# A conditioned two-layer decoder step: x loaded ahead of the first modulation weights, softmax's masked copy scaled by -1/8 with a minimum that starts at the negated sink, and another block order

## The chip, the cores and the metric

One Trainium2 chip, one of its cores. The metric is the device time of one execution in microseconds. A core has TensorE (PE, the matrix products; "PEld" is its weight load), VectorE (DVE), ScalarE (ACT), GpSimd (POOL), a queue engine SyncE (SP) that here only starts transfers, and 16 DMA engines that carry the transfers between HBM and the on-chip memory SBUF. Products land in PSUM, eight banks of 2 KB per partition.

## The reference, cut to what matters

512 prompt tokens and 8 x 8 sample tokens go through two layers of width 1024, in float32.

```python
for l in range(DEPTH):                       # DEPTH = 2
    sh1, sc1, g1, sh2, sc2, g2 = split(silu(c) @ ada_w[l] + ada_b[l], 6)
    h = rms_norm(x, norm_g[l, 0]) * (1 + sc1) + sh1
    out = recurrent_block(h, ...) if l < 1 else attention(h @ attn_w_q, k, v) @ attn_w_o
    x = x + g1 * out
    h = rms_norm(x, norm_g[l, 1]) * (1 + sc2) + sh2
    x = x + g2 * swiglu(h, ffn_w_in[l], ffn_w_out[l])
    if l == 0: k, v = shared keys and values from the modulated norm of x
y = rms_norm(x, final_g)
```

Recurrent block: `xr, yg = split(h @ w_in)`, a causal convolution of width 4 on `xr`, two sigmoid gates from 8 blocks of 128 x 256, a linear recurrence with `a = exp(8 r log_sigmoid(lambda))`, times `gelu(yg)`, `@ w_out`. Attention: 16 heads of 64 over 4 key heads, a window of 128, and a learned sink in the softmax:

```python
s = where(mask, q @ k.T / 8, -1e30)
m = maximum(max(s), sink)
p = exp(s - m) / (sum(exp(s - m)) + exp(sink - m))
```

## The kernel before

**Tiling.** The 576 tokens are two halves of 288 (256 prompt and 32 sample tokens), A (h = 0) and B (h = 1), with features on the partitions, eight columns c of 128 features. Each float32 operand is split into a rounded high part and the low rest, so a block of 128 x 128 weights times a half is three products of 128 x 288 (high-high, high-low, low-high). Weights come as units of 512 KB into `raw` buffers; ScalarE copies the high part, VectorE subtracts for the low part (buffers `wh`). `x0` to `x7` are the units of `rnn_w_in`'s first half, `y0` to `y7` of the second, `g0` to `g7` the gates of block c.

**Order.** The program is recorded first: each engine call is an entry with a cost from a table (`Engine.record`), and `Recorder.schedule` puts the entries in an order per engine by those costs. All entries are issued from one line, L447, so every row of the profile has that line. The strings `RNN` and `ATT` give the order in which the blocks of the recurrent layer and of attention are recorded (q: query columns, a: attention of a chunk of prompt heads, s: one sample's attention, f: its end, o: output columns; A and B are the halves). `early(n)` moves an entry n places up in priority.

**Front.** SP's queue loads c, x (tile 4 is the samples, tiles 0 to 3 the prompt), vectors and weights in the recorded order. `x_half` squares and sums x for the norm and turns its tiles by transposes on TensorE. `ada_first(c)` computes shift and scale (SH1, SC1) of the first layer for two columns: 32 matmuls of 128 columns into an `ada` bank, from 2 MB of `ada_w` that `ada_first_load` brings, a copy, a transpose, `ada_end` for bias and gain (`mods`). Then `modulated` makes `x * rstd` (VectorE and GpSimd), scales and shifts it (ScalarE, into `tb`), and splits it into `h`. Four such stages of two columns follow each other; tiles 2 and 3 of x are loaded behind the first stage's weights. The other modulations are computed later, spread among the products, in 512-wide matmuls from `reg` buffers. `decay_rates` computes log_sigmoid of lambda on VectorE by powers of two and series.

**Softmax.** `attn_chunk(c)` takes two heads (j) and two token blocks (b) of a half. Scores are masked and their maximum found by one reduction on VectorE; then follow the scaled minimum with the negated sink (`nm`), the sink's exponent argument, Exp on ScalarE with its sum, and the division. `attn_sample` does it for one sample with the sink as an extra column.

Of the kernel before, what the change touches and what calls it, by code (L numbers as in the profile page):

```python
# [12 lines left out]
F32 = mybir.dt.float32  # L13
# [26 lines left out]
ST = (1, 1, 1)  # L40
EW = EP = EA = EK = E1 = ER = 0
# [11 lines left out]
ATT = ("q0A a0A q1A q2A q0B a1A q1B a0B a2A q3A q2B a1B a3A q3B q4A q4B a2B q5A a4A a3B q6A a5A q5B a4B "  # L53
       "q7A a6A q6B a5B s0A s1A a7A s2A s3A q7B s0B a6B fA a7B o0A s1B s2B o1A s3B o2A fB")
# [324 lines left out]
class Engine:  # L379
# [8 lines left out]
    def record(self, name, args, kw):  # L388
# [18 lines left out]
        if name == "matmul":  # L407
# [9 lines left out]
            if first.ap[0][1] == 32 and args[1].ap[0][1] == P and n >= P:  # L417
                cost = n / 2.4 + 30 if dt == F32 else n / 9.6 + 15
                mode = 3
        elif name == "transpose":  # L420
            cost = 107.0
        elif name == "dma_start":
            src = args[1]
            n = max(_free(first) * first.ap[0][1], _free(src) * src.ap[0][1])
            cost, lat = (460.0 if eng == "SP" else 1020.0), n * 4 / 335.0 + 5
# [21 lines left out]
        self.rec.add(eng, lambda: getattr(obj, name)(*map(real, args), **{k: real(v) for k, v in kw.items()}), cost, outs, ins, func, lat, port, mode)  # L447

# [25 lines left out]
def trunk_kernel(ctx, tc, a):  # L474
# [123 lines left out]
    for t in (4, 0, 1):  # L598
        x_load(t)
# [44 lines left out]
    def decay_rates():  # L644
        tw = sl()
        z, neg, msk, scl, p_, w_, w2, s_ = [tw.f[:, 8 * i : 8 * i + 8] for i in range(8)]
        V.tensor_scalar(hgb[:], vecT[:, 80:96], 0.5, None, ALU.mult)
        V.tensor_scalar(neg, lamT, -1.0, None, ALU.mult)
        V.tensor_tensor(z, lamT, neg, ALU.max)
        V.tensor_scalar(z, z, 87.0, None, ALU.min)  # L650
        V.memset(scl, 1.0)
        for kk in (64, 32, 16, 8, 4, 2, 1):
            V.tensor_scalar(msk, z, kk * math.log(2.0), None, ALU.is_ge)
            V.scalar_tensor_tensor(z, msk, -kk * math.log(2.0), z, ALU.mult, ALU.add)
            V.tensor_scalar(w_, msk, -1.0, 1.0, ALU.mult, ALU.add)
            V.scalar_tensor_tensor(w_, msk, 2.0 ** -kk, w_, ALU.mult, ALU.add)
            V.tensor_tensor(scl, scl, w_, ALU.mult)
        V.memset(p_, 1.0)
        for n in range(11, 0, -1):
            V.scalar_tensor_tensor(p_, p_, -1.0 / n, z, ALU.mult, ALU.mult)  # L660
            V.tensor_scalar(p_, p_, 1.0, None, ALU.add)
        V.tensor_tensor(p_, p_, scl, ALU.mult)
# [4 lines left out]
        V.memset(s_, 1.0 / 17)  # L667
        for n in range(15, 0, -2):
            V.tensor_tensor(s_, s_, w2, ALU.mult)
            V.tensor_scalar(s_, s_, 1.0 / n, None, ALU.add)  # L670
        V.scalar_tensor_tensor(s_, s_, 2.0, w_, ALU.mult, ALU.mult)
        V.scalar_tensor_tensor(s_, neg, 0.0, s_, ALU.max, ALU.add)
# [20 lines left out]
    def ada_turn(o, n):  # L693

        t = aux()
# [20 lines left out]
    def ada_first_load(c, kind):  # L716

        first_w[c] = []
        for q in range(4):
            b = kind(F32) if kind is whs else kind()  # L720
            first_w[c].append(b)
            for g in (SH1, SC1):
                w, o = ada_w(g)
                src = w[q * 2 * P : (q + 1) * 2 * P, o + c * P : o + (c + 2) * P].rearrange("(k p) n -> p k n", p=P)
                Q.dma_start(b.f[:, 512 * g : 512 * g + 512].rearrange("p (k n) -> p k n", k=2), src)

    def ada_first(c):
        o = ps(pada, "ada")
        for q, b in enumerate(first_w[c]):
            for k in range(2):  # L730
                ada_mm(o, 2 * q + k, [b.f[:, n : n + P] for n in (256 * k, 256 * k + P, 512 + 256 * k, 512 + 256 * k + P)], q + k == 0, q + k == 4)
            b.done()
        t = ada_turn(o, 1)[:, 0:P].rearrange("p (g c b) -> p g c b", g=2, c=2)
        for g in (SH1, SC1):
            ada_end(g, slice(c, c + 2), t[:, g, :, 0:9])
# [1266 lines left out]
```

## Time and profile before

| | |
|---|---|
| median of 3 runs | 1262.42 us (1261.84 to 1265.04) |
| the profiled execution's own time | 1263.01 us |
| its span | 1261.2 us |
| TensorE busy | 1237.8 us |
| VectorE, ScalarE, GpSimd busy | 920.3, 663.1, 252.7 us |
| moved by DMA | 165.38 MB, mean 131 GB/s |

A row of the timeline has start, duration, engine, line, operation, output <- inputs by the program's names, shape, count, and in brackets the idle time ahead of it with what ended it. A window's row has the stretch, then for PE, PEld, DVE, ACT and POOL the busy time and number of instructions, then the granted TensorE clock, the DMA engines' busy share and GB/s. A row of groups has the count, busy time, mean ns of one, and idle time before. A row of waits has the total, the number and the longest. Matmuls are pipelined and their ends are modelled, so times of single ones overlap; the starts are measured.

### The profile page before, as it was taken

The page shows a single profiled execution, that of the slowest core. Times are in us where ns is not written, and L with a number is a line of the kernel's source. Part 1 is how long each engine was busy: PE and PEld are TensorE (multiplying, and loading weights), DVE is VectorE, ACT ScalarE, POOL GpSimd, SP SyncE. Part 2 cuts the span into 40 slices and gives each one's busy share as a digit, 9 for nine tenths or more (in the row PEclk, how much of TensorE's full clock was granted, in tenths as well). Part 3 has the DMA queues.
Part 4 walks back from the last instruction along what each step waited for, and adds up shares of the span by engine and source line. Part 5 has one row for each costly group of instructions (what it writes and reads, how often), then busy time and mean ns, then how long its engine had stood idle before and what let it go on. Part 6 is the DMA issues. An engine that isn't in the chain of part 4 may idle for free.

```text
span 1261.2 us, 25276 instructions
## 1 busy us (share of the span) xinstructions
PE 1237.8 (98%) x9532; PEld 1166.9 (93%) x9532; DVE 920.3 (73%) x2283; ACT 663.1 (53%) x1498; POOL 252.7 (20%) x542
## 2 busy tenths in 40 slices
PE   7999999999999999999999999999999999999997
PEld 5798999899899899989998997999999999999997
DVE  6998784795577468656778887558957865875776
ACT  4788973764255335514567678538523542552442
POOL 3456351101100010011024335100011011001011
PEclk8999999999999999999999999999999999999999
DMA  9955554535456655464513220332342232332322
GB/s 306 318 179 188 188 177 151 170 86 171 140 152 191 185 167 184 156 194 137 167 33 75 68 60 27 111 97 97 85 133 68 84 110 76 90 100 80 100 69 76
DMA packets 219755, 165.38 MB, mean 131 GB/s; under 512 B 23629, under 2 KB 204841, under 8 KB 219602
## 3 DMA queue, kind: packets, MB, share of 16 engines
q1 hardware_dynamic: 219186, 163.45, 43.0%
q8 instruction: 75, 1.23, 0.4%
q0 software_dynamic: 448, 0.32, 0.1%
q14 instruction: 46, 0.38, 0.1%
HBM read 160.85 MB, written 4.87 MB: 131 GB/s over the span
## 4 chain that ended last, share of the span: by engine, by line
PE 86%; DVE 6%; ACT 4%; DMA 2%; POOL 1%; issue 1%; SPq 0%; ACTq 0%; DVEq 0%
PE mm L447 82%; PE ada L447 4%; DVE wh L447 1%; DVE ta L447 1%; ACT tb L447 1%; DVE sl L447 1%; ACT ta L447 1%; DVE tb L447 1%; ACT h L447 1%; DMA raw<-in_rnn_w_in_dram 1%; ACT wh L447 1%; POOL h L447 1%; DMA reg<-in_ada_w_dram 1%; ACT sl L447 1%; DMA reg<-in_x_prompt_dram 1%
## 5 line engine op out<-in xcount | busy, mean ns | idle before, releaser
L447 PE MATMUL mm<-h,wh 128*128 128x288 f32 x4128 | 596.2, 298 | 3.8 <-ACT h L447 1.8
L447 PEld LDWEIGHTS mm<-h,wh 128*128 128x128 f32 x4128 | 560.5, 188 | 23.2 <-issue 11.3
L447 PE MATMUL mm<-sl,wh 128*128 128x288 f32 x3218 | 460.6, 296 | 0.4 <-ACT sl L447 0.3
L447 ACT CAST wh<-raw 128x512 fp32r<-128x512 f32 (+2 forms) x380 | 269.1, 721 | 345.7 <-PE mm L447 208.9
L447 PEld LDWEIGHTS mm<-sl,wh 128*128 128x128 f32 x3218 | 436.6, 188 | 9.0 <-issue 5.9
L447 DVE TENSOR_TENSOR wh<-raw,wh 128x512 fp32r<-128x512 f32 (+2 forms) x380 | 310.2, 828 | 59.3 <-ACT wh L447 57.0
L447 DVE SCALAR_TENSOR_TENSOR x<-mm,mods,x 128x256 f32<-128x256 f32 x160 | 77.0, 482 | 136.1 <-PE mm L447 136.0
L447 POOL TENSOR_TENSOR td<-td,td 128x288 f32<-128x288 f32 x38 | 35.5, 934 | 475.8 <-ACT td L447 467.7
L447 POOL TENSOR_TENSOR x<-x,ta 128x32 f32<-128x32 f32 x152 | 55.3, 364 | 331.1 <-DVE ta L447 325.9
L447 PE MATMUL mm<-tb,wh 128*128 128x288 f32 (+1 forms) x488 | 88.5, 296 | 0.4 <-ACT td L447 0.4
L447 PEld LDWEIGHTS mm<-tb,wh 128*128 128x128 f32 x488 | 72.4, 188 | 1.9 <-DVE sl L447 0.8
L447 ACT COPY td<-mm 128x288 f32<-128x288 f32 (+2 forms) x140 | 49.0, 364 | 37.7 <-DVE mm L447 18.0
L447 DVE TENSOR_TENSOR raw<-raw,raw 128x512 f32<-128x512 f32 x76 | 61.4, 808 | 0.9
L447 PE MATMUL mm<-ta,wh 128*128 128x288 f32 (+1 forms) x254 | 56.1, 298 | 0.0
L447 ACT ACTIVATE ta<-x 128x288 f32<-128x288 f32 x56 | 24.8, 444 | 55.6 <-POOL x L447 52.4
L447 DVE TENSOR_TENSOR raw<-raw 128x512 f32<-128x512 f32 x76 | 52.2, 688 | 1.1
L447 DVE TENSOR_TENSOR td<-mm,td 128x288 f32<-128x288 f32 x76 | 34.5, 454 | 23.4 <-PE mm L447 23.3
L447 PE MATMUL ada<-reg,cz 128*32 128x512 f32 (+1 forms) x448 | 49.5, 553 | 0.0
L447 PEld LDWEIGHTS mm<-ta,wh 128*128 128x128 f32 x254 | 41.7, 188 | 1.8 <-ACT wh L447 0.8
L447 ACT ACTIVATE ta<-ta,stat 128x128 f32<-128x128 f32 (+2 forms) x72 | 32.3, 471 | 18.5 <-DVE stat L447 17.7
L447 DVE TENSOR_TENSOR acc<-acc,ta 128x288 f32<-128x288 f32 x54 | 25.1, 464 | 12.4 <-ACT ta L447 12.4
L447 ACT CAST sl<-ta 128x288 fp32r<-128x288 f32 x54 | 23.0, 431 | 18.5 <-DVE ta L447 18.5
(202 smaller groups left out, 1197.9 us busy)
## 6 DMA issues: line engine op xcount, KB each, us to landing
raw<-in_ffn_w_in_dram SPq DMA_DIRECT2D x88, 512.0 KB
reg<-in_ada_w_dram SPq DMA_DIRECT2D x80, 512.0 KB
raw<-in_ffn_w_out_dram SPq DMA_DIRECT2D x48, 384.0 KB
raw<-in_rnn_w_in_dram SPq DMA_DIRECT2D x16, 512.0 KB
reg<-in_kv_ada_w_dram SPq DMA_DIRECT2D x16, 512.0 KB
wh<-in_ada_w_dram SPq DMA_DIRECT2D x24, 256.0 KB
raw<-in_rnn_w_out_dram SPq DMA_DIRECT2D x8, 512.0 KB
raw<-in_ffn_w_out_dram SPq DMA_DIRECT2D x8, 512.0 KB
```

The lines of the kernel that those rows point to most:

```text
L447: self.rec.add(eng, lambda: getattr(obj, name)(*map(real, args), **{k: real(v) for k, v in kw.items()}), cost, outs, ins, func, lat, port, ...
```

## The change

1. **x first.** All five tiles of x are loaded and turned ahead of the first modulation weights, and `X0` holds `x * rstd` for all columns before shift and scale are known (`modulated` then runs with `known=True`).
2. **The first modulation in three stages** (`FIRST`): columns 0 to 3 at once from 4 MB in rows of 2 KB, 32 matmuls of 256 columns, then columns 4 and 5, and 6 and 7, as before. The matmuls of a stage stay together by `FQ`. Their transposes go to the `ada` banks.
3. **Units.** x0 to x3 are loaded as pairs of two columns by half the rows (`unit_two`, rows of 1 KB), and the gates as two units of four blocks instead of two units by gate (`ug`). `linear_two` is the product over such a pair.
4. **Decay rates** by ScalarE's Exp and a shorter series.
5. **Softmax.** The reduction adds the mask, scales by -1/8, and takes the minimum from the negated sink on, so it gives `nm` directly; Exp then has scale -1. The sink's argument for both token blocks is one subtraction.
6. **Another order**: `ATT`, the recorder's costs of narrow float32 matmuls and of transfers by row length, and priorities (`E1`).

SP's queue at the start (`wh_` and `reg_` are buffers; the last figures are partitions, blocks and columns), before:

```order
L447 DMA reg_108<-in_x_sample_dram 64x1024
L447 DMA reg_111<-in_x_prompt_dram 128x1024
L447 DMA reg_113<-in_x_prompt_dram 128x1024
L447 DMA sl_116<-in_ada_b_dram 96x128
L447 DMA sl_118<-in_norm_g_dram 32x128
L447 DMA wh_121<-in_ada_w_dram 128x2x256 x2
L447 DMA wh_127<-in_ada_w_dram 128x2x256 x2
L447 DMA wh_137<-in_ada_w_dram 128x2x256 x2
L447 DMA wh_147<-in_ada_w_dram 128x2x256 x2
L447 DMA raw_160<-in_rnn_w_in_dram 128x8x128
L447 DMA reg_166<-in_x_prompt_dram 128x1024
```

and after:

```order
L453 DMA reg_107<-in_x_prompt_dram 128x1024
L453 DMA reg_109<-in_x_prompt_dram 128x1024
L453 DMA reg_112<-in_x_prompt_dram 128x1024
L453 DMA reg_114<-in_x_prompt_dram 128x1024
L453 DMA sl_117<-in_ada_b_dram 96x128
L453 DMA sl_120<-in_norm_g_dram 32x128
L453 DMA raw_124<-in_rnn_w_in_dram 128x4x256
L453 DMA wh_131<-in_ada_w_dram 128x2x512
L453 DMA wh_135<-in_ada_w_dram 128x2x512
L453 DMA wh_140<-in_ada_w_dram 128x2x512
L453 DMA wh_146<-in_ada_w_dram 128x2x512
```

Two tiles of x and the first weight unit moved ahead of the modulation weights; the first stage's eight loads are of 512 KB instead of 256 KB.

TensorE around the first products (`mm_349`, `mm_441` and `mm_444` are their PSUM banks, `h_` the modulated half A; `ada_` rows with `cz` are modulation matmuls, rows with `ident` transposes), before:

```order
L447 MATMUL ada_214<-wh_147,cz 32x128 x6
L447 MATMUL mm_308<-ident,ta_304 128x128
L447 MATMUL mm_285<-ident,sl_163 128x96
L447 MATMUL mm_331<-ident,reg_166 128x128 x4
L447 MATMUL mm_337<-ident,reg_166 128x128 x4
L447 MATMUL mm_349<-h_323,wh_314 128x288
L447 MATMUL mm_354<-ident,reg_173 128x128 x4
L447 MATMUL mm_362<-ident,reg_173 128x128 x4
```

and after:

```order
L453 MATMUL ada_302<-wh_166,cz 32x256 x2
L453 MATMUL ada_302<-wh_173,cz 32x256 x2
L453 MATMUL mm_357<-ident,sl_180 128x64
L453 MATMUL ada_393<-ident,ta_385 128x128 x2
L453 MATMUL ada_415<-reg_183,cz 32x128 x8
L453 MATMUL ada_415<-reg_201,cz 32x128 x8
L453 MATMUL mm_441<-h_432,wh_265 128x288
L453 MATMUL mm_444<-h_432,wh_265 128x288
```

Before, one product stands between the transposes of x's tiles 2 and 3, after two columns are modulated; now four columns are, and half of the next stage's modulation matmuls stand ahead of the first product.

VectorE in the first softmax chunk (`stat` holds `nm`, `snk` the sinks; ISA rows are the reduction and the read of its accumulator), before:

```order
L447 ISA ta_9075,stat_96<-mm_9045,reg_7886 128x256
L447 ISA stat_96 128x1
L447 SCALAR_TENSOR_TENSOR stat_96<-stat_96,snk 128x2
L447 ISA tb_9083,stat_96<-mm_9047,reg_7886 128x256
L447 ISA stat_96 128x1
L447 TENSOR_TENSOR stat_96<-stat_96,snk 128x2
```

and after:

```order
L453 ISA ta_8975,stat_96<-mm_8951,reg_7616,snk 128x256
L453 ISA stat_96 128x1
L453 ISA tb_8980,stat_96<-mm_8953,reg_7616,snk 128x256
L453 ISA stat_96 128x1
L453 ISA ta_8985,stat_95<-mm_8961,reg_7616,snk 128x128
```

The scaled minimum and the addition between the reductions are gone, and the reductions read the negated sink.

The diff, cut:

```diff
-ST = (1, 1, 1)
+ST = (2, 1, 2)
+FQ = ((0, 1), (2,), (3,))
+FIRST = ((0, 4), (4, 2), (6, 2))
+E1 = ((400, 200), (0, 0), (0, 0))
-ATT = ("q0A a0A q1A q2A q0B a1A q1B a0B a2A q3A q2B a1B a3A q3B q4A q4B a2B q5A a4A a3B q6A a5A q5B a4B "
-       "q7A a6A q6B a5B s0A s1A a7A s2A s3A q7B s0B a6B fA a7B o0A s1B s2B o1A s3B o2A fB")
+ATT = ("q0A q1A a0A a1A q2A q0B q1B q2B a0B q3A a2A q4A a3A a1B q3B a2B q5A a4A q4B a3B q6A a5A q5B a4B "
+       "q7A a6A s0A q6B a7A s1A s2A s3A a5B q7B s0B a6B fA o0A s1B a7B s2B s3B o1A fB o2A")
...
-    for t in (4, 0, 1):
+    for t in (4, 0, 1, 2, 3):
         x_load(t)
...
+        V.tensor_tensor(p_, lamT, neg, ALU.min)
+        S.activation(p_, p_, AF.Exp)
...
+    def linear_two(us, col, ops, evac):
+        def run(h):
+            o = ps()
+            product(o[:, 0:HC], us[0], ops(h)[0:4], last=False, col=col)
+            product(o[:, 0:HC], us[1], ops(h)[4:8], first=False, col=col)
...
-                    V.tensor_tensor_reduce(out=y[:, 0:W], in0=sc[j][:, 256 * b : 256 * b + W], in1=masks[:, 256 - W : 256], op0=ALU.add, op1=ALU.max,
-                                           scale=1.0, scalar=-1e30, accum_out=mx[:, 2 * b + j : 2 * b + j + 1])
-                V.scalar_tensor_tensor(nm[:, i], mx[:, i], -0.125, nsink[:, 2 * c : 2 * c + 2], ALU.mult, ALU.min)
-                V.tensor_tensor(mx[:, i], nm[:, i], sinks[:, 2 * c : 2 * c + 2], ALU.add)
+                    V.tensor_tensor_reduce(out=y[:, 0:W], in0=sc[j][:, 256 * b : 256 * b + W], in1=masks[:, 256 - W : 256], op0=ALU.add, op1=ALU.min,
+                                           scale=-0.125, scalar=nsink[:, 2 * c + j : 2 * c + j + 1], accum_out=nm[:, k : k + 1])
...
+        X0[h] = [sl() for _ in range(KC + 1)]
+        V.tensor_tensor(X0[h][KC].f[:, 0 : 32 * KC].rearrange("p (c n) -> p c n", c=KC), x[h][:, :, HP:HC], rstd[h][:, HP:HC].unsqueeze(1).to_broadcast([P, KC, 32]), ALU.mult)
+        for c in range(KC):
+            (V, V, G)[c % 3].tensor_tensor(X0[h][c].f[:, 0:HP], x[h][:, c, 0:HP], rstd[h][:, 0:HP], ALU.mult)
...
     x_half(0)
-    ada_first_load(0, whs)
+    x_half(1)
+    load_more(1)
+    ada_first_load(*FIRST[0], whs)
     vectors()
```

168 lines of the change are left out of this document (89 added, 79 removed).

## The prediction

> **What bounds the kernel now.** I read first the page's busy shares and its chain, then the windows of the first 70 us, then TensorE's own timeline there, because the chain says that TensorE is the path almost everywhere.
>
> ```profile
> PE 1237.8 (98%) x9532; PEld 1166.9 (93%) x9532; DVE 920.3 (73%) x2283; ACT 663.1 (53%) x1498; POOL 252.7 (20%) x542
> ...
> PE 86%; DVE 6%; ACT 4%; DMA 2%; POOL 1%; issue 1%; SPq 0%; ACTq 0%; DVEq 0%
> ...
> 245.61 49.69 PE mm L447 x371
> ```
>
> TensorE is busy for 98% of the span, and in a quiet stretch of the chain 371 products take 49.69 us, 0.134 us each. From about 50 us to the end it is fed without pause, so a change can win only where it is not fed: at the start, at a few stage borders, and in attention. The windows give each engine's busy time in 10 us, the granted clock, the DMA share and GB/s:
>
> ```profile
> 0.00:10.00 10.00, 4.69 (x27) 4.17 (x28) 0.97 (x6) 5.10 (x8) 6.12 (x20) 1.00 0.76 234
> 10.00:20.00 10.00, 6.74 (x84) 4.11 (x83) 8.64 (x39) 3.09 (x7) 2.50 (x6) 1.00 1.11 336
> 20.00:30.00 10.00, 9.91 (x84) 7.08 (x82) 8.90 (x31) 6.37 (x14) 2.09 (x5) 0.66 1.11 346
> 30.00:40.00 10.00, 8.01 (x103) 5.50 (x103) 9.27 (x44) 5.07 (x13) 3.08 (x4) 1.00 1.13 327
> 40.00:50.00 10.00, 10.00 (x105) 7.50 (x106) 9.18 (x55) 6.17 (x15) 1.66 (x2) 1.00 1.10 338
> 50.00:60.00 10.00, 9.79 (x72) 7.73 (x71) 9.50 (x25) 9.20 (x27) 5.13 (x13) 1.00 0.97 287
> ```
>
> The DMA engines are full from 10 to 50 us, VectorE is at nine tenths throughout, and TensorE's clock is low between 20 and 30. TensorE's rows of that stretch (start, duration, what, count):
>
> ```profile
> 16.40 0.63 PE L447 MATMUL ada<-wh,cz 128*32 128x128 f32 x12
> ...
> 20.71 0.61 PE L447 MATMUL mm<-h,wh 128*128 128x288 f32 x1
> ...
> 29.14 0.64 PE L447 MATMUL ada<-wh,cz 128*32 128x128 f32 x16
> ...
> 34.81 0.66 PE L447 MATMUL mm<-h,wh 128*128 128x288 f32 x3 [1.57 <-ACT h L447]
> ...
> 46.98 0.63 PE L447 MATMUL ada<-wh,cz 128*32 128x128 f32 x12
> ...
> 56.87 1.93 PE L447 MATMUL ada<-reg,cz 128*32 128x512 f32 x16
> ...
> 74.54 1.93 PE L447 MATMUL ada<-reg,cz 128*32 128x512 f32 x16
> ```
>
> The first product starts at 20.71 and the last columns of the first modulation at 46.98. The second block of 512-wide modulation starts at 74.54; in both orders exactly 237 products stand before it. It is my finish line for the front. Between 20.71 and 74.54 lie 53.8 us for 31.7 us of products (237 x 0.134): the rest is modulation, x's transposes, waits and slow clock.
>
> **The change, part by part.** First the front's start. Ahead of the first product now stand x (0.26 + 4 x 0.52 MB), one weight unit (0.52) and eight modulation loads of 0.52: 7.1 MB, with some 0.3 of vectors 7.4 (before: 4.3). By the windows 2.34 + 3.36 = 5.70 MB pass in 20 us, and the other 1.7 at 346 GB/s need 4.9: 24.9 us. The same count puts the last byte of before's first unit (4.25 MB) at 15.7, and the chain has it landed at 10.72 + 7.41 = 18.13, 2.4 later:
>
> ```profile
> 10.72 7.41 DMA raw<-in_rnn_w_in_dram
> ...
> 28.00:29.00 1.00, 1.00 (x20) 0.77 (x19) 1.00 (x6) 1.00 (x4) 0.00 (x0) 1.00 1.10 354
> ...
> 31.00:32.00 1.00, 0.83 (x18) 0.63 (x18) 0.93 (x6) 0.12 (x1) 0.42 (x1) 1.00 1.18 305
> ...
> 48.00:49.00 1.00, 1.00 (x10) 1.00 (x9) 0.93 (x9) 0.87 (x1) 0.00 (x0) 1.00 1.01 410
> ```
>
> So the last quarter lands at 27.3 if the rate stays. It need not: by the byte count the 28th us carried rows of 1 KB (354 GB/s), the 31st rows of 512 B (305), the 48th rows of 4 KB (410). The change makes the first modulation's rows 2 KB and those of units x0 to x3 and of the gates 1 KB instead of 512 B. At 380, between the two neighbours, the landing is 25.8. I take 26.5; both ends go into the range. The last quarter's 8 matmuls of 256 columns are half of 8 of 512 (1.93 at 56.87), so 1.0: end 27.5. In before the last modulation ended at 17.03 and the first product came 3.7 later, ScalarE's 1.04 us conversion among it; that conversion is now done in the wait, while two more small VectorE steps are added, so 3.4: first product at 30.9 (29.8 to 32.5), ten later than before. Who was waiting on the moved loads: SP's queue now puts x's last two tiles and the unit ahead of all modulation. The unit's load also waits there for a buffer that ScalarE's square of tile 0 frees, and the modulation behind it; over 2 MB of x are then still in flight, so I price that at nothing; with the queue run dry it would be about 1 us.
>
> Then to the finish line: 237 products 31.7; 64 small modulation matmuls (before: 128), 8 per 0.64 (row 29.14, where the profile has two records for each), 5.1, of which 1.3 stands ahead of the first product: 3.8; the first 512-wide block 1.9; transposes 0.4. Sum 37.8, so 68.7 with no wait. x's last transposes and the normalization of x, which stood between products, are hidden under the wait for 4.2 MB. Waits I add: ScalarE feeds two columns in 1.6 us,
>
> ```profile
> 35.11 1.09 ACT L447 ACTIVATE tb<-ta,mods 128x256 f32<-128x256 f32 x2
> 36.11 0.70 ACT L447 CAST h<-tb 128x256 fp32r<-128x256 f32 x2
> 36.71 1.05 ACT L447 CAST wh<-raw 128x1024 fp32r<-128x1024 f32 x1
> ```
>
> (35.11 to 36.71), and 12 products on them take 1.6: even, so about 0.7 for the sample columns. Ahead of columns 4 and 5, ScalarE then has two conversions of 1.05 (row 36.71) and VectorE their two lo parts; VectorE does the second lo part ahead of the step that columns 4 and 5 wait for. Products of other columns cover all but about 1.2. The evacuations of four units at once cost 0.5, a half clock about 0.4. Together 2.8: finish line at 71.5 against 74.54, **gain 3.0**. Ends: 29.8 + 37.8 + 1 = 68.6 (gain 5.9), and 32.5 + 37.8 + 5.7 = 76.0 (loss 1.5), the 5.7 being the 2.8, 1.3 more of half clock and 1.6, as much as the longest wait on ScalarE above (1.57 at 34.81).
>
> What removes the cover of VectorE's decay chain: 80 tiny instructions in three groups, 13.7 us busy,
>
> ```profile
> L447 DVE TENSOR_SCALAR sl<-sl 128x8 f32<-128x8 f32 x35 | 5.8, 166 | 0.3
> ...
> L447 DVE SCALAR_TENSOR_TENSOR sl<-sl 128x8 f32<-128x8 f32 x27 | 4.9, 183 | 0.5
> ...
> L447 DVE TENSOR_TENSOR sl<-sl 128x8 f32<-128x8 f32 x18 | 3.0, 164 | 0.4
> ```
>
> become about 15 of them, roughly 11 us off an engine that was full; no term of its own, it is why I let VectorE keep pace above. ScalarE takes one Exp and a table load, in the wait. Later the order has three table loads fewer (22 to 19), beside full TensorE: 0; were TensorE not fed there, they would be a gain. The split gate units hold two buffers instead of four: 0 for the same reason. The transposes of the first modulation go from the six product banks to the other two: 0, with the products as cover. POOL's queue issues the same loads in the same place. The units of x0 to x3 come as pairs by rows, so x0 and x1 need a second load for columns 4 to 7; it lands after the first half's 48 products can start, and the wait for it is in the 1.2 above.
>
> Softmax: per pair of blocks two scaled minima and two additions go, one addition comes; 40 + 32 - 16 = 56 small ones by 0.187 take 10.4 us off VectorE.
>
> ```profile
> L447 DVE SCALAR_TENSOR_TENSOR stat<-stat,snk 128x2 f32<-128x2 f32 (+1 forms) x40 | 7.1, 183 | 0.0
> ...
> L447 DVE TENSOR_TENSOR stat<-stat,snk 128x2 f32<-128x2 f32 x32 | 6.0, 191 | 0.4
> ...
> 59.79 0.47 DVE L447 TENSOR_TENSOR tb<-sl,ta 128x300 fp32r<-128x300 f32 x1
> 60.17 0.53 DVE L447 SCALAR_TENSOR_TENSOR sl<-td,vecT,sl 128x300 f32<-128x300 f32 x1
> ```
>
> The 72 reductions now read a per-partition start value. No row shows that; the nearest, an instruction with such an operand against one without, is 0.53 to 0.47, so 0.06 each or 4.3 us back; ends 0 and 0.3 (five times that row). TensorE's waits from 640 to 812 us:
>
> ```profile
> PE mm L447 <- DVE wh L447: 1.0, 1, 1.0
> PE mm L447 <- ACT ta L447: 0.8, 1, 0.8
> ...
> PE ada L447 <- ACT td L447: 0.3, 1, 0.3
> ...
> PE mm L447 <- DVE td L447: 0.5, 2, 0.3
> PE mm L447 <- ACT td L447: 0.4, 2, 0.2
> PE mm L447 <- ACT h L447: 0.2, 1, 0.2
> PE mm L447 <- ACT wh L447: 0.2, 1, 0.2
> ```
>
> These are 3.4 us. The first two stand before softmax and stay. A shorter VectorE chain and the new order (a5B and q7B now after the A samples) can take the rest, and unflagged thin spots around 770 to 792 as much again. I take **1.3**; ends 3 and, since an order can also expose a chain, -1.
>
> Sum 4.3 on the profiled execution's 1263.0: 1258.7. That execution stands 0.6 above the median 1262.42, so 1258.1.
>
> [...] The row first: TensorE's granted clock fell to 0.50 after a sparse stretch and came back in the 28th us.
>
> ```profile
> 18.00:19.00 1.00, 0.00 (x0) 0.00 (x0) 0.90 (x5) 0.84 (x1) 0.63 (x2) 1.00 1.05 357
> ...
> 21.00:22.00 1.00, 1.00 (x6) 1.00 (x6) 1.00 (x4) 1.00 (x3) 0.00 (x0) 0.50 1.12 342
> ...
> 27.00:28.00 1.00, 1.00 (x18) 0.50 (x12) 0.93 (x6) 0.37 (x2) 0.00 (x0) 0.81 1.10 351
> ```
>
> The wait for 4.2 MB is longer and sparser: four bursts of 1 us in 17 to 27 us. [...]
>
> **Rivals.** [...] (b) *All covered*: the landing at 25.8 and waits of 1.0: front 5.5, attention 2.4, time 1254.5. For it: 38 us of work for TensorE lie ready between 31 and 69 us. Against: three engines must keep an even pace for that. (c) *It moves the start and not the end*: VectorE (9.50 of 10 from 50 to 60) sets the finish line through conversions and evacuations: gain 0, time 1262.4. Against: 11 us fewer there. (d) *Slower*: the reductions' start value turns them into a slower form. At 0.3 each VectorE gains 21.6 in the attention stage and loses 10.4; it becomes late for the transposes' copies and TensorE waits for most of the 11: 1262.4 - 3.0 + 10 = 1269.4. It decides from about 0.145 each on (10.4 / 72), and the time passes that of before at about 0.19. Against it: the 0.06.
>
> **How the numbers follow.** 0.3% of 1262.4, what a measurement here can tell from no change, is 3.8: faster means under 1258.6, slower over 1266.2. Forecast 0.50, own range 1255.5 to 1260.5, of which 0.30 lie under 1258.6 and 0.20 above; (b) 0.22; (a) 0.15; (c) 0.06; (d) 0.07. Faster 0.30 + 0.22 = 0.52; same 0.20 + 0.15 + 0.06 = 0.41; slower 0.07. The range goes from (b) less 1.0, for both upper ends at once, to (c) plus 0.6, the spread of one execution: 1253.5 to 1263.0.
>
> **What would show it.** Right: first product at 30 to 32.5, the second 512-wide block at 70 to 73, no wait over 1.5 between; decay instructions a quarter; attention's waits under 3 us; the reduction's mean 0.43 at most for 256 columns by the same row kind. Wrong: a first product after 34, clock 0.50 beyond 33, or a wait on VectorE in the first 70 us above 2.

## The result and the profile after

| | before | after |
|---|---|---|
| median | 1262.13 us (1261.72 to 1265.04, 4 runs) | 1253.72 us (1253.59 to 1254.91, 4 runs) |
| ratio | | 0.9931, 95% interval 0.9913 to 0.9948 |
| profiled execution, span | 1263.01, 1261.2 | 1253.59, 1251.6 |

The change is faster by 8.4 us, which is 0.7% and clear of the noise. The forecast gain was 4.3, about half of it; the time lies at the lower end of the range. First the page of the changed kernel, the busy shares and the chain by engine:

```profile
PE 1229.2 (98%) x9468; PEld 1164.5 (93%) x9468; DVE 907.7 (73%) x2144; ACT 657.4 (53%) x1492; POOL 260.6 (21%) x541
...
PE 93%; DVE 4%; ACT 2%; issue 0%; POOL 0%; DMA 0%; ACTq 0%; SPq 0%
```

TensorE is 93% of the chain instead of 86%. VectorE and ScalarE fell from 10% of it to 6, DMA from 2% to 0. Where that happened is seen in the windows of the first 60 us (PE, PEld, DVE, ACT, POOL, then granted clock, DMA share, GB/s):

```profile
10.00:20.00 10.00, 6.82 (x41) 4.96 (x44) 9.46 (x20) 5.38 (x9) 4.53 (x8) 0.81 1.07 365
20.00:30.00 10.00, 8.33 (x97) 4.13 (x90) 9.18 (x44) 3.16 (x10) 1.03 (x3) 0.85 1.08 361
30.00:40.00 10.00, 10.00 (x120) 8.89 (x120) 6.20 (x16) 8.37 (x22) 2.02 (x5) 1.00 1.10 349
40.00:50.00 10.00, 10.00 (x100) 9.63 (x100) 5.65 (x18) 8.09 (x25) 2.30 (x7) 1.00 1.09 360
50.00:60.00 10.00, 10.00 (x77) 8.30 (x76) 9.96 (x20) 9.57 (x22) 8.73 (x15) 1.00 0.90 287
```

From 30 to 50 us TensorE has no gap, and VectorE is busy for 6.20 and 5.65 of 10 us, where before it was 9.27 and 9.18. ScalarE is busier than before: 8.37 and 8.09 instead of 5.07 and 6.17. TensorE's own rows give the milestones: the last quarter of the first modulation, the first product, and the two 512-wide blocks of which the second is the finish line:

```profile
25.06 1.06 PE L453 MATMUL ada<-wh,cz 128*32 128x256 f32 x12 [0.58 <-DMA wh<-in_ada_w_dram]
...
29.25 1.40 PE L453 MATMUL mm<-h,wh 128*128 128x288 f32 x7 [0.60 <-ACT h L453]
...
51.79 1.92 PE L453 MATMUL ada<-reg,cz 128*32 128x512 f32 x16
...
67.83 1.92 PE L453 MATMUL ada<-reg,cz 128*32 128x512 f32 x16
```

The first product starts 8.5 us later than before, the finish line comes 6.7 us earlier. The later stages can be cut where half A's sums for a norm start (six or four matmuls of one column): behind layer 0, behind attention, and before the end. Before:

```profile
643.11 0.73 PE L447 MATMUL mm<-small,acc 128*128 128x1 f32 x6
...
843.57 0.69 PE L447 MATMUL mm<-small,acc 128*128 128x1 f32 x6
...
1235.48 0.56 PE L447 MATMUL mm<-small,acc 128*128 128x1 f32 x4
```

After, the last two of them (the first is at 635.24):

```profile
834.67 0.69 PE L453 MATMUL mm<-small,acc 128*128 128x1 f32 x6
...
1225.32 0.56 PE L453 MATMUL mm<-small,acc 128*128 128x1 f32 x4
```

So the stages of one traced execution each, in us, for all kernels that were run ("layer 0" is the finish line to 643.11, "attention" is with keys and values):

| kernel | front | layer 0 | attention | last feed-forward | end | median |
|---|---|---|---|---|---|---|
| before | 74.54 | 568.57 | 200.46 | 391.91 | 25.7 | 1262.13 |
| before again (e8) | 73.99 | 568.54 | 201.34 | 391.85 | 25.8 | 1262.63 |
| after | 67.83 | 567.41 | 199.43 | 390.65 | 26.3 | 1253.72 |
| after again (e12) | 70.47 | 567.40 | 199.33 | 390.63 | 26.4 | 1254.01 |
| e1 x late | 72.10 | 569.23 | 199.58 | 390.64 | 25.6 | 1258.83 |
| e2 narrow stages | 71.00 | 567.85 | 199.11 | 391.11 | 25.6 | 1256.48 |
| e3 old decay rates | 72.69 | 568.99 | 198.99 | 391.68 | 25.7 | 1258.86 |
| e4 old softmax | 69.77 | 567.34 | 206.32 | 390.93 | 25.6 | 1261.07 |
| e5 old ATT | 68.03 | 567.40 | 216.92 | 390.58 | 25.6 | 1270.67 |
| e6 old costs | 68.71 | 569.58 | 199.16 | 392.19 | 25.6 | 1257.79 |
| e7 old units | 71.16 | 568.66 | 199.63 | 391.81 | 25.5 | 1258.48 |
| e9 old softmax and ATT | 67.71 | 567.37 | 203.22 | 390.99 | 25.6 | 1254.88 |
| e10 before, new softmax | 75.89 | 569.43 | 213.98 | 392.11 | 25.6 | 1277.75 |
| e11 before, new decay | 73.77 | 571.18 | 200.51 | 391.34 | 25.6 | 1264.18 |
| e13 after, filled | 68.14 | 567.56 | 199.22 | 390.70 | 26.3 | 1254.10 |
| e14 before, filled | 73.07 | 569.00 | 200.40 | 391.54 | 25.8 | 1262.49 |
| e15 after, 1 KB rows | 69.93 | 567.38 | 199.04 | 390.63 | 25.6 | 1254.10 |
| e16 after, VectorE late | 71.22 | 567.37 | 199.14 | 390.62 | 25.6 | 1255.45 |

The 9.6 us between the two spans are 6.7 in the front, 1.2 in layer 0, 1.0 in attention, 1.3 in the last feed-forward, less 0.6 at the end. The second traces of the two kernels (e8 and e12) give 3.5 in the front and the same in layer 0 and the feed-forward. Layer 0 and the feed-forward repeat within 0.1 us when a kernel is run again; the front of the changed kernel does not (67.8 and 70.5, see e12), so single fronts of kernels that differ by under 2.6 us are not told apart, and medians are used there.

### The profile page after: what moved, and what is told of

It reads as the page before. It is cut to its first block, busy times and chain, and to the rows that moved or that the text cites. A ratio compares the mean times of both kernels' runs of the same rounds, so it can differ in the third digit from the quotient of the medians.

```text
span 1251.6 us, 25018 instructions
## 1 busy us (share of the span) xinstructions
PE 1229.2 (98%) x9468; PEld 1164.5 (93%) x9468; DVE 907.7 (73%) x2144; ACT 657.4 (53%) x1492; POOL 260.6 (21%) x541
## 4 chain that ended last, share of the span: by engine, by line
PE 93%; DVE 4%; ACT 2%; issue 0%; POOL 0%; DMA 0%; ACTq 0%; SPq 0%
PE mm L453 88%; PE ada L453 5%; DVE sl L453 1%; ACT h L453 1%; DVE tb L453 1%; DVE wh L453 0%; ACT tb L453 0%; DVE ta L453 0%; ACT ta L453 0%; POOL h L453 0%; ACT wh L453 0%; DVE stat L453 0%; DVE x L453 0%; DVE h L453 0%; DMA raw<-in_c_sample_dram 0%
## 5 line engine op out<-in xcount | busy, mean ns | idle before, releaser
L453 ACT ACTIVATE ta<-ta,stat 128x256 f32<-128x256 f32 (+2 forms) x72 | 32.4, 472 | 14.6 <-DVE stat L453 14.1
L453 DVE TENSOR_TENSOR acc<-acc,ta 128x288 f32<-128x288 f32 x54 | 25.2, 467 | 12.5 <-ACT ta L453 12.5
```

## The experiments

The kernel after was timed with the result and in e12, the kernel before beside every run; its median moved from 1262.1 to 1263.5 us. So a loss told below as a difference of medians can be up to 1 us smaller by the ratio to before, and the intervals of e2, e9, e13, e15 and e16 overlap both of the kernel after. e1 to e3 and e6, e7 undo one part of the change each; e4, e5, e9 and e10 are about attention; e8 and e12 repeat the two kernels; e11 does one part alone; e13 to e16 hold the planned order and move one thing.

### e1: x's tiles 2 and 3 behind the first stage's weights

```diff
-    for t in (4, 0, 1, 2, 3):
+    for t in (4, 0, 1):
...
-    x_half(1)
     load_more(1)
     ada_first_load(*FIRST[0], whs)
     vectors()
+    for t in (2, 3): x_load(t)
+    x_half(1)
```

> The changed kernel (1253.7 us) with x's tiles 2 and 3 loaded and turned behind the first stage's 4.2 MB of modulation weights, as before, all else kept. Theory F (the gain is the front: x out of the way and the first products fed without a wait, 6.7 us by the second 512-wide block): half B's operands come later and x's transposes and norm steps fall between products again, second 512-wide block at 69.5 to 71.5 instead of 67.8, time 1255.5 to 1257.5. Theory V (the gain is VectorE's relief by the shorter decay chain and softmax, and the place of x is of no account): block within 0.7 us of 67.8, time 1253 to 1254.5.

1258.83 us, ratio 0.9964 (0.9951 to 0.9976): 5 us of the gain are gone, more than expected. 1.8 of them are layer 0 under another order (569.23 us). TensorE's waits in its first 80 us:

```profile
PE ada L453 <- DMA wh<-in_ada_w_dram: 2.5, 5, 0.7
...
PE mm L453 <- DVE wh L453: 0.9, 2, 0.5
```

The modulation starts early and starves by pieces. Its last weights are there at 22.05 us, 3 us before those of the kernel after, but x's last tiles are then turned between modulation and products, and the first product comes at 30.12. Half B's normalization now falls between products, where VectorE gets late (0.9, a wait that the kernel after does not have).

### e2: four stages of two columns, x still first

```diff
-FIRST = ((0, 4), (4, 2), (6, 2))
+FIRST = ((0, 2), (2, 2), (4, 2), (6, 2))
```

> The changed kernel with the first modulation in four stages of two columns (rows of 1 KB) instead of four columns at once (rows of 2 KB); x still first. Theory F with row length: the first product comes 4 to 6 us earlier (2.1 MB less ahead of it), but the 4.2 MB take 12.0 instead of 10.8 us, 32 more small matmuls cost TensorE 2.3 us less 4.0 of wide ones ahead, and small waits return: second 512-wide block at 68.5 to 70, time 1254.5 to 1256. Theory V: no change, 1253 to 1254.5.

1256.48 us, 0.9948 (0.9935 to 0.9962). TensorE's first product and, behind it, its waits in the first 80 us:

```profile
25.31 1.26 PE L453 MATMUL mm<-h,wh 128*128 128x288 f32 x5 [1.48 <-ACT h L453]
```

```profile
PE mm L453 <- ACT h L453: 2.9, 2, 1.5
PE mm L453 <- DVE wh L453: 1.6, 1, 1.6
```

The products start 4 us earlier than in the first trace of the kernel after, but with two columns at hand they wait for ScalarE and VectorE, and the median is some 2.6 us longer (all five runs, from 1256.15 on, lie above all nine of the kernel after). The early start bought nothing, because the feed did not keep up.

### e3: the old decay rates

```diff
-        V.tensor_tensor(p_, lamT, neg, ALU.min)
-        S.activation(p_, p_, AF.Exp)
+        ... the 80 instructions of before
```

> The changed kernel with the long decay computation on VectorE (80 small instructions more or less) put back. Theory V: about 11 us more of VectorE in the front, TensorE waits for conversions and modulated columns: second 512-wide block at 70.5 to 72, time 1256.5 to 1258. Theory F: VectorE was only about 0.6 busy between 30 and 50 us after the change, so it hides nearly all of it: block at 68 to 69, time 1253.7 to 1255.

1258.86 us, 0.9965 (0.9953 to 0.9978): 5 us lost. The timeline, VectorE's first shift in the kernel after, then the same and the first product in e3:

```profile
27.06 0.43 DVE L453 TENSOR_TENSOR mods<-ada,abT 128x18 f32<-128x18 f32 x4
```

```profile
29.41 0.42 DVE L453 TENSOR_TENSOR mods<-ada,abT 128x18 f32<-128x18 f32 x4
...
31.59 1.55 PE L453 MATMUL mm<-h,wh 128*128 128x288 f32 x4 [2.71 <-ACT h L453]
```

The first half of the chain stands ahead of the modulation's end on VectorE. The weights were there as early as in the kernel after (last quarter at 24.99), yet shift and scale came 2.35 us later, and so the first product. The other half, about 40 small instructions, falls among the products, as the windows show:

```profile
30.00:40.00 10.00, 8.41 (x65) 6.89 (x66) 7.97 (x29) 8.89 (x21) 2.32 (x9) 0.66 1.10 348
40.00:50.00 10.00, 10.00 (x121) 8.88 (x120) 8.44 (x46) 5.60 (x15) 1.52 (x2) 1.00 1.07 357
```

VectorE is busy for 7.97 and 8.44 of 10 us there, yet no product behind the first has a marked wait. From first product to finish line it takes 41.1 us instead of 38.6; the clock was half up to 36.9 us, over 5.3 us of it, which is a loss of some 2.6. So in this trace the chain costs by its place ahead of the first shift, and not by the load that it puts on VectorE afterwards.

### e4 and e5: one half of the attention change undone

```diff
(e4)  reduction by maximum, scaled minimum and addition as before
(e5)  -ATT = ("q0A q1A a0A a1A q2A q0B ...
      +ATT = ("q0A a0A q1A q2A q0B a1A ...
```

> The changed kernel with the softmax of before (maximum, then scaled minimum and addition) put back, block order kept. Theory V: VectorE is late in attention, from the norm ahead of it to the norm behind it (181.25 us after the change) 183 to 185 us, time 1255.5 to 1257.5. Theory F: TensorE is fed there anyway, 181 to 182.3 us, time 1253.5 to 1255.

> The changed kernel with the block order of attention of before. Theory O (the order is what shortened attention by 1.2 us): norm ahead of attention to the norm behind it 182 to 183.5 us instead of 181.25, time 1254.5 to 1256. Theory S (softmax did it): 181 to 181.7 us, time 1253.3 to 1254.2.

e4 1261.07 us, 0.9979 (0.9971 to 0.9988); e5 1270.67, 1.0061 (1.0047 to 1.0075). Attention loses 6.9 and 17.5 us: each half alone is worse than neither. The biggest waits of e5 between 690 and 862 us, and the window in which its clock was lowest:

```profile
PE mm L453 <- ACT h L453: 2.9, 2, 1.6
PE mm L453 <- DVE stat L453: 1.9, 3, 0.8
PE mm L453 <- POOL ta L453: 1.4, 1, 1.4
```

```profile
815.00:820.00 5.00, 3.41 (x10) 2.38 (x10) 1.92 (x4) 0.83 (x3) 0.00 (x0) 0.50 0.00 0
```

All waits in its table there sum to 9.2 us (2.0 in the kernel after's). The other half is the clock: it was below full between 785 and 795 and between 810 and 825, 8.5 us of clock in all. Both low stretches begin beside long stalls, 1.27 us ahead of the product at 787.58 and 1.45 ahead of the transpose at 813.59, and the products behind them ran slow as well. That the stalls brought the low clock is not shown: e8 and e9 have it there too, with no stall over 0.25 us near. In e4 (the same view) the waits are shorter, and the clock stayed at 1.00 from 662 to 852 us:

```profile
PE mm L453 <- DVE td L453: 1.7, 3, 0.9
PE mm L453 <- DVE stat L453: 1.5, 4, 0.5
```

e4's marked waits there sum to 4.7 us, 2.7 more than the kernel after's, so more than half of its 6.9 carries no mark.

### e6: the old costs in the planner

```diff
-                cost = n / 2.2 if dt == F32 else n / 9.6 + 15
+                cost = n / 2.4 + 30 if dt == F32 else n / 9.6 + 15
...
-  n * 4 / (250.0 if pk <= 512 else 308.0 if pk <= 1024 else 345.0) + 5
+  n * 4 / 335.0 + 5
```

> The changed kernel with the recorder's old costs for narrow float32 matmuls and for transfers; the program computes the same, only the order of instructions can differ. Theory C (part of the gain, above all the 1.2 us in the recurrent and first feed-forward layer and the 1.2 us in the second, comes from an order that fits the durations better): time 1254.7 to 1257, with the loss spread over the stages. Theory F: within 0.8 us, 1253.0 to 1254.5.

1257.79 us, 0.9955 (0.9943 to 0.9968). Layer 0 and the last feed-forward are 2.2 and 1.5 us longer than after. One wait of TensorE of before's comes back in each (waits, 75 to 643 and 862 to 1225 us):

```profile
PE mm L453 <- ACT sl L453: 0.3, 1, 0.3
PE mm L453 <- DVE td L453: 0.2, 1, 0.2
...
PE mm L453 <- ACT td L453: 0.4, 1, 0.4
```

In the kernel after both tables are empty. The program computes the same, so the order that the new costs give is a part of the gain, far from the front.

### e7: the old units

`ug`, `pair` and `linear_two` as before (units of all rows, gates by gate).

> The changed kernel with x0 to x3 and the gates as whole units of 512 B rows again. Theory F with row length: 6 units at about 305 instead of 349 GB/s are 1.3 us more of full DMA before 50 us, but x0 then needs one unit and not two before all its columns can go; second 512-wide block at 67.8 to 69.3, time 1253.7 to 1255.5. Theory R (the split units are the point, since two units serve 96 products of the first four columns): block at 70 or later, time 1256 or more.

1258.48 us, 0.996 (0.9948 to 0.9973). From the first product (30.37) to the finish line it takes 40.8 us instead of 38.6, and layer 0 and the feed-forward are 1.2 us longer each, as before: again the order of the whole has changed, so the price of the units by themselves is not shown.

### e8: the kernel before, again

> The kernel before, unchanged, for a second trace: how far the milestones (second 512-wide block 74.54, norms at 643.11, 843.57 and 1235.48 us) move between executions of one program. If by under 0.3 us, the small gains of 1.2 us after the front are the program's; if by about 1 us, they are not to be told from the execution.

1262.63 us, 0.9998 (0.9988 to 1.0008). Its stages are in the table; attention's 201.34 has a stretch of low clock that the first trace has not (0.66 between 785 and 790), the rest repeats within 0.6. It is the same program, and TensorE's longest wait from 775 to 790 us is 0.25 in both traces.

### e9 and e10: old softmax and old ATT together; new softmax alone

e9 is the kernel after with both halves of e4 and e5, e10 the kernel before with the new softmax.

> The kernel after with both the old softmax and the old order of attention blocks; front, units, decay rates and costs stay new. Theory 'a pair': the order and the reduction are fitted to each other, and either pair is nearly as good as the other; attention then takes 182.5 to 183.2 us as in the kernel before (181.25 after; 188.2 and 198.8 with one half undone), and the time is 1253.7 + 1.5 = 1255.2 us. Rival 'the new costs changed what fits': the old pair under the new costs loses as the half-undone kernels did, attention over 186, time over 1258. The front has the same instructions as the kernel after: first product between 29.2 and 31.1 us, second 512-wide block between 67.8 and 69.8, as its two runs so far spread.

> The kernel before with the new softmax alone (old order of blocks, old costs, old front). Theory 'a pair': the new softmax under the old order loses as it did in the kernel after with the old order (17.5 us): attention near 198, time near 1278 us. Rival 'the work counts': 56 small VectorE instructions fewer, 10 us of VectorE, are worth 0 to 2 us by themselves: attention 181 to 183, time 1260.5 to 1262.5. In between, the loss is one of how the recorded costs happen to place the blocks, and neither half has a price of its own.

e9 1254.88 us, 0.9942 (0.993 to 0.9955), 0.9 slower than the kernel after timed beside it (1254.01), where the two intervals overlap. Its traced attention is longer than its median tells, with a half clock from 778 to 785 (the traced execution took 1256.65; the other four took 1254.61 to 1258.59). e10 1277.75, 1.0116 (1.0102 to 1.013), with the same waits as e5 to the tenth of a us for `h`, `stat`, `ta` of GpSimd and `td`. So the new softmax loses under the old order with the new front and costs and with the old ones, and the new pair is worth about 0.9 over the old one, a size that the noise nearly covers.

### e11: the new decay rates alone, in the kernel before

> The kernel before with the short decay rates alone. Theory 'the chain stands ahead of the modulation': the long chain stood between the small steps that end each modulation stage on VectorE, so without it the finish line of the front (second 512-wide block, 74.5 and 74.0 us in two runs) comes 2 to 3.5 us earlier, near 71.5, and the time is 1259.5 us. Rival 'the old front waits for data': the modulation weights set the pace there, finish line 73.5 to 74.5, time 1262.2 us.

1264.18 us, 1.0007 (0.9998 to 1.0016): no gain. The front ends at 73.77, near before's 73.99 and 74.54, and layer 0 is 2.6 us longer, most of it one wait (TensorE's waits, 110 to 222 us):

```profile
PE mm L447 <- ACT ta L447: 1.9, 1, 1.9
```

So the short chain gained nothing in the old front, while undoing it in the new one cost 5 us (e3). The likely reason, not tested by itself, is that VectorE is the last one there only where x and the weights are early enough.

### e12: the kernel after, again

> The kernel after once more, for how far its front and its stages repeat. If they repeat as those of the kernel before did: first product 28.7 to 29.9 us, second 512-wide block 67.2 to 68.5, norm behind layer 0 at 634.6 to 635.9, time 1253.7 us. If the landing of the last modulation weights varies as the kernel with the old softmax suggested: first product up to 31.1, second block up to 69.8, time up to 1255.7 us in single runs.

1254.01 us (1253.65 to 1255.93), 0.9927 (0.9913 to 0.994). The traced execution is the longest, 1255.93. TensorE's timeline and one window of it:

```profile
26.20 1.92 PE L453 MATMUL ada<-wh,cz 128*32 128x256 f32 x12 [2.17 <-DMA wh<-in_ada_w_dram]
...
31.50 1.67 PE L453 MATMUL mm<-h,wh 128*128 128x288 f32 x7 [0.36 <-ACT h L453]
```

```profile
30.00:31.00 1.00, 1.00 (x24) 0.64 (x16) 0.93 (x4) 1.00 (x3) 0.00 (x0) 0.50 1.09 348
```

The last weights came 1.1 us later than in the first trace. The clock was half from 18.9 to 22.3 us and again from 25.8 to 32.6: the last quarter took 1.92 instead of 1.06, and the first 1.1 us of products ran slow. So the half clock came over the first products, which is what the chances count as (a), in part and in one execution, at 1255.93 us; the other eight of this kernel took 1253.59 to 1254.91.

### e13 and e14: TensorE's idle time filled ahead of the low clock

```diff
(e13, in spread; e14 the same with 12 ahead of x's tile 2)
+                    for _ in range(20):
+                        nc.tensor.transpose(real(pt_[:, 0:P]), ident[:], ident[:])
                     run()
```

> The kernel after with 20 more transposes of the identity (2.7 us) in TensorE's idle stretch of 3.2 us ahead of the first modulation (from 14.3 us), written to a bank that is overwritten right behind them; order and everything else are unchanged. [...]

> The kernel before with 12 more transposes of the identity (1.6 us) in TensorE's idle stretch of 1.75 us ahead of x's tile 2 (from 17.8 us); order and everything else are unchanged. Theory 'the old half clock was paid for': its 3.4 us of lost clock between 20.8 and 27.8 us fell on products and transposes, and without it the second 512-wide block comes 1.5 to 3 us before 74.0 to 74.5, median near 1260.5. [...]

e13 1254.1 us, 0.9934 (0.9921 to 0.9946); e14 1262.49, 0.9994 (0.9985 to 1.0003). The fill of e13 in the timeline and two windows of e13:

```profile
13.72 2.40 PE L829 MATMUL mm<-ident 128*128 128x128 f32 x20
```

```profile
19.00:20.00 1.00, 0.93 (x20) 0.27 (x8) 1.00 (x2) 0.32 (x1) 1.00 (x2) 1.00 1.06 389
...
26.00:27.00 1.00, 0.83 (x5) 0.47 (x3) 0.67 (x4) 0.37 (x1) 0.05 (x1) 0.50 1.10 349
```

The low clock from 16.2 to 23.0 us is gone (it was 0.50 in the 20th us); a shorter low stretch comes at 25.2 to 28.6, and the median stays. One run of e13 is still at 1255.94. In e14 the low stretch from 20.6 to 27.4 is gone, and its finish line came at 73.07, where the theory had 71 to 73:

```profile
22.00:23.00 1.00, 1.00 (x9) 0.77 (x8) 1.00 (x3) 0.61 (x2) 0.00 (x0) 1.00 1.10 344
```

The time differs by 0.2 of 1262.70 us, within its interval, and is not near the theory's 1260.5. So in the medians neither kernel pays a measurable price for the low clock at its start; the one traced front of e14 is 0.9 to 1.5 us shorter than the two of before.

### e15: the same bytes in rows of 1 KB

```diff
+                        for i in range(2):
+                            nc.sync.dma_start(real(dst[:, :, 256*i : 256*i+256]), src[:, :, 256*i : 256*i+256])
```

> The kernel after with each of the eight loads of the first modulation stage split into two, so that the same 4.2 MB come in rows of 1 KB instead of 2 KB; the order and the computation are unchanged. Theory 'row length set the landing': rows of 1 KB pass at 350 GB/s and rows of 2 KB at 389 in the traces so far, so 4.2 MB take 12.0 instead of 10.8 us; the last quarter starts 1.2 us later (26.3 instead of 25.06), first product at 30.5, median 1255 (more, up to 1256.5, where the half clock then reaches the products). Rival 'the queues' depth counts, not the row': under 0.4 us, median 1253.7 to 1254.1.

1254.1 us, 0.9931 (0.9917 to 0.9944). The window of the 17th us, after and then e15, and e15's last quarter:

```profile
16.00:17.00 1.00, 0.00 (x0) 0.00 (x0) 1.00 (x5) 0.00 (x0) 0.39 (x1) 0.59 1.05 387
```

```profile
16.00:17.00 1.00, 0.00 (x0) 0.00 (x0) 1.00 (x4) 0.00 (x0) 0.72 (x1) 0.98 1.10 349
```

```profile
26.23 1.80 PE L453 MATMUL ada<-wh,cz 128*32 128x256 f32 x12 [1.18 <-DMA wh<-in_ada_w_dram]
```

The rates, 387 and 349 GB/s, are as expected. The last quarter starts 1.17 us later than in the first trace of the kernel after, but in e12 the unchanged kernel has it at 26.20 too, so one landing does not tell the two theories apart. The median is the rival's: the same as after's by the ratio to before (0.9931 to 0.9927), where I expected 1255. In the traced execution the front ends 2.1 us later than in the first trace of after, but attention is 0.4 and the end 0.7 shorter, so its span is 1.0 longer (1252.6); the other runs' fronts were not traced.

### e16: VectorE late by 2.4 us, order held

```diff
+            for _ in range(12):
+                nc.vector.tensor_scalar(real(w_), real(w_), 1.0, None, ALU.mult)
```

> The kernel after with 12 more tiny VectorE instructions (about 2.4 us) inside the short decay chain, ahead of the first shift and scale; the order is unchanged. [...] Rival 'the changed order of the rest made most of the 5 us': second block at 68 to 70, time 1254 to 1256.

1255.45 us, 0.9942 (0.993 to 0.9955), 1.4 more than the kernel after's 1254.01 and 1.35 more than e13 and e15, which were timed beside it. VectorE's added instructions and first shift, and TensorE's first product:

```profile
24.58 2.44 DVE L675 TENSOR_SCALAR sl<-sl 128x8 f32<-128x8 f32 x12
...
29.28 0.42 DVE L453 TENSOR_TENSOR mods<-ada,abT 128x18 f32<-128x18 f32 x4
```

```profile
31.45 2.05 PE L453 MATMUL mm<-h,wh 128*128 128x288 f32 x7 [2.82 <-ACT h L453]
```

First shift and first product come as late as in e3, and layer 0 and the feed-forward keep the kernel after's 567.4 and 390.6. The finish line, 71.22, is later than the rival's 68 to 70 and 1.5 us ahead of e3's; the time is the rival's. So of e3's 5 us, about 1.4 are the delay ahead of the first product with some half clock behind it (31.3 to 34.8 us in this trace), and 2.6 are layer 0 (568.99) and the feed-forward (391.68) under another order. Some 1 is left; in e3's trace the half clock lies over 2 us more of the products, which would be about that much, but one trace of each does not settle it.

## Why the prediction was half right

**What the sum missed.** By the first two traces the front gained 6.7 us where 3.0 were forecast, layer 0 and the last feed-forward 2.4 where nothing was, attention 1.0 where 1.3 were, and the end lost 0.6. The 2.4 repeat in the second traces; the front's share does not (3.5 there).

**The start: right in kind, forecast too late.** The row lengths did what the bytes said: 378 to 393 GB/s at 2 KB (after, 12 to 23 us), where 380 was taken. The last quarter was forecast to land at 26.5, halfway between two bounds; it started at 25.06 and 26.20 in the two traces. The first product, forecast at 30.9 (29.8 to 32.5), came at 29.25 and 31.50, so once below the lower bound; that is 1.65 us of the first trace's front.

**The first failing step: the waits between the first product and the finish line.** The prediction put 2.8 us there, on top of 37.8 of work: 0.7 for the sample columns, 1.2 for columns 4 and 5 behind conversions, 0.5 for evacuations, 0.4 for a half clock. From first product to finish line it took 38.6 us in the first trace, 39.0 in the second and 38.6 in e13: 0.8 to 1.2 above the 37.8, and no wait mark on any product behind the first. The work itself was priced about 1 us too high. By the starts of its rows the first trace has 3.2 us of modulation matmuls behind the first product (3.8 taken) and under 0.1 of transposes (0.4 taken). So the 237 products took some 1.8 us more than 237 x 0.134, in pieces too short for a mark.

The slack of VectorE, 6.20 and 5.65 of 10 us, suggests itself as the reason, but e3 does not bear it out: there VectorE is at 7.97 and 8.44, and the products still have no marked wait. Nor did ScalarE get slack. What e2 and e1 show is where the feared waits on `h` and on `wh` do come: in kernels whose products start before four columns are ready, or while x is still to be normalized. Why each of the four terms came out smaller was not tested one by one. No run shows the 0.4 of half clock, nor the 1.3 more of it in the late end, 76.0: they were the author's estimates. In the first trace the clock is 1.00 from 23 us on and so over all the products, in e13 it is back at 28.6, ahead of the first product (29.57), and in e12 0.50 over the first 1.1 us of them, which would be some 0.6 lost.

This is the course of rival (b), all covered, and the time came out 0.8 below the 1254.5 that it gave. That nearness is partly luck: (b) had 5.5 in the front and 2.4 in attention, and nothing for the other stages.

**The second failing step: the terms put at 0 "beside full TensorE".** The prediction held that TensorE is fed without pause from about 50 us on, so that table loads, split units and another order would be worth nothing in layer 0 and the feed-forwards. Layer 0 is 1.16 and the last feed-forward 1.26 us shorter, and they repeat so in e12. TensorE was not quite fed there: before has marked waits of 0.3 and 0.4 on ScalarE (TensorE's waits, 75 to 643 and 862 to 1225 us),

```profile
PE mm L447 <- ACT sl L447: 0.3, 1, 0.3
...
PE mm L447 <- ACT td L447: 0.4, 1, 0.4
```

and after has none. The other 0.9 and 0.9 carry no mark, but counting from start to start finds where they lie: the same 3801 products of 288 columns take 510.35 us of layer 0 in before and 508.93 in after, the same 2905 of the feed-forward 388.40 and 387.13 (the second traces agree to 0.1). So it is time between products of the same work. e6, which changes nothing but the planner's costs, loses both gains; e3 and e7 lose them too, e1 loses that of layer 0 and e2 part of both. e4, e5, e9 and all kernels with a held order keep them. So they hang on the planned order, not on one part of the change; which wait each order avoids stays open.

**Attention: right in size, wrong in kind.** Forecast 1.3, traced 1.0, and 0.9 in the medians of e9 against e12. But the prediction expected it from TensorE's waits of 3.4 us, which should fall below 3. They did not: over attention the marked waits sum to 3.6 us in before and 4.3 in after (3.5 and 3.9 in the second traces). The two largest in after (635 to 862 us):

```profile
PE mm L453 <- ACT ta L453: 2.5, 4, 1.1
PE mm L453 <- DVE wh L453: 1.3, 2, 1.0
```

What became shorter is small matmuls: from start to start the same 150 of 128 x 128 take 16.1 instead of 17.2 us, and the rest differs by some tenths up or down. And the prediction counted VectorE's saving and the order as two helps that add up, with a loss of 1 us at most if the order exposes a chain. e4, e5 and e10 show a lock and its key: either alone costs 7 to 17 us.

**The unknown price: right.** The reduction with a per-partition start value was bounded at 0 to 0.3 us and taken as 0.06 from the row of another instruction. Groups of 128 x 256 between 690 and 862 us, before and after:

```profile
L447 DVE CUSTOM_DVE_ANT_0 ta<-mm,reg 128x256 f32<-128x256 f32 x24 | 10.0, 418 | 3.3 <-PE mm L447 3.2
```

```profile
L453 DVE CUSTOM_DVE_ANT_0 ta<-mm,reg,snk 128x256 f32<-128x256 f32 x24 | 11.4, 478 | 2.5 <-PE mm L453 2.5
```

418 to 478 ns, 0.060 each. It decides the other way only from 0.145 on, so rival (d) fell. The mean of "0.43 at most" by which the prediction would have known it was a slip: with its own 0.06 it should have said 0.48.

**The other rivals.** (c), the start moves and not the end, fell with the finish line; e2 is a kernel in which an earlier start brought a later end. (a), a half clock over the first products, was half true: it came in one of the two traced executions of the kernel after (e12, 0.50 up to 32.6 us). What brings the low clock is not shown. In e13, filling 2.4 us of TensorE's idleness put off the low stretch by some 9 us (from 16.2 to 25.2). In e8 and e9 the clock fell at 786 and 778 us with no wait of TensorE over 0.25 us in the 10 us before. Nor is it shown what ends it: the low stretch lasted 3.4 us in e13 and 6.8 in e12, the latter with TensorE busy for most of it.

**The end** is 0.6 us longer in both traces of the kernel after and in e13, and 25.6 in most others. The trace puts it behind the last store: from the end of its issue to the end of the span it takes 4.9 us in after, 4.4 in before and 4.2 in e15. Why stays open.

## What to carry to other kernels

A wait that shows in the kernel before need not survive a change in what is ready when the products start: price it again for the new order, and let the range lean that way. Here a late start that found four columns and all of x ready beat an early start that was fed in pieces (e1, e2). TensorE, 98% busy, still held 0.9 us in each of two stages in gaps too short for a wait mark: before putting a stage at 0, compare what its like products take from start to start with what they take in a quiet stretch. Parts that were fitted together (a block order, its costs, an instruction's length) have no price of their own: undoing them one by one here cost 2.6 to 17 us each, against 8.4 for all. To learn what one part costs in a planned program, hold the order and change only that part; otherwise the new plan's 1 to 3 us stand in the answer.

## What the runs showed of the hardware

- Two traced executions of the kernel after, 1253.59 and 1255.93 us (e12), differ by their start: the last quarter started at 25.06 and 26.20 us, the clock was at 0.50 only ahead of the products (16.2 to 23.0) or also over the first of them (25.8 to 32.6), and the finish line came at 67.83 and 70.47. The other stages agree within 0.1.
- The clock was low late in the program too. In e5 it fell twice in attention, to 0.50 between 815 and 820 us; the two stretches began beside stalls of TensorE of 1.27 and 1.45 us and took 8.5 us of clock, nearly as much as the 9.2 us of waits. In e8 and e9 it fell at 786 and 778 us beside waits of at most 0.25, while the first trace of before, the same program as e8, ran that place at 1.00.
- The first modulation stage's loads, 4.2 MB in both, passed at 345 to 350 GB/s in rows of 1 KB (e15, 13 to 23 us) and at 378 to 393 in rows of 2 KB (after, 12 to 23 us).
